# One program order for ScalarE, VectorE and PE through the expert part of a two-layer encoder

## The chip, the cores and the metric

The kernel is one program on one core of a Trainium2 chip. The metric is device time in microseconds from launch to end, the median over runs. Before the change it is 1147.02 us, the median of 3 runs (1145.33 to 1148.85).

Five engines matter. PE (TensorE) multiplies matrices and puts the results into the eight banks of PSUM; its weight loads are listed as PEld. ACT (ScalarE) and DVE (VectorE) copy, cast and combine tiles. SP (SyncE) issues the DMAs that bring data from device memory into SBUF. POOL (GpSimd) does little here. Each engine has its own list of instructions and takes them in the order in which the built program has them; an instruction that needs another engine's result waits on a semaphore, and all behind it on that engine wait with it.

## The reference

Two transformer layers over 256 tokens of width 1024, in float32: an even one (gated linear attention beside differential attention, then a SwiGLU feed-forward part), and an odd one (latent attention, then a mixture of eight SwiGLU experts). Only the odd layer's second half, the experts, is touched by the change:

```python
def _moe_swiglu(x, router_w, w_gate, w_up, w_down):
    t = x.reshape(B * S, D)                                  # 256 x 1024
    logits = (t @ router_w).astype(jnp.float32)
    top_vals, top_idx = lax.top_k(logits, TOP_K)             # 2 of 8
    w = jax.nn.softmax(top_vals, axis=-1)
    combine = jnp.einsum('nk,nke->ne', w, jax.nn.one_hot(top_idx, N_EXPERTS, dtype=jnp.float32))
    out = jnp.zeros_like(t)
    for e in range(N_EXPERTS):                               # w_gate, w_up 1024 x 2816, w_down 2816 x 1024
        out = out + combine[:, e:e + 1].astype(t.dtype) * _swiglu(t, w_gate[e], w_up[e], w_down[e])
    return out.reshape(B, S, D)
```

where `_swiglu(x) = (silu(x @ w_gate) * (x @ w_up)) @ w_down`. A layer norm over `ALPHA * x + out` follows and is the kernel's output.

## The kernel before, in words

**The experts as rounds.** The kernel sorts the experts by how many tokens chose them. The four fullest are *wide* (up to 128 token rows), the others *narrow* (up to 64). One-hot matrices P, made on DVE from the router's ranks (`one_hot`), gather each expert's rows on PE (`gather_pair`, `gather_narrow`; tiles ga, gn, xw, xn), and their transposes PT scatter the results back (`pt`, `e_scatter`, `n_tail`; tiles pt, sc, ns). Each expert's weights come as 33 chunks of 128 x 2048 floats (1 MB): 11 each of gate, up and down. The hidden width is done in six blocks b. The loop in `expert_steps` runs over rounds r: a round does block b of a wide expert (gate and up products, `e_gu`, tiles eg and eu), the down products of the wide block before (`e_down`, tile ey), the transposes of the hidden values (`e_tr`, `e_hT`: et, ehT), and then, two rounds behind (`BEHIND`), a narrow expert's blocks (`n_gu`, `n_down`, `n_tr`, `n_hT`: ng, nu, ny, nt). A full round takes six wide and six narrow chunks.

**The split.** A wide chunk is cut into a high part wh, rounded to the matmul's fast 32-bit form by a cast on ACT (helper line 126, CAST wh<-raw), and the rest wl, a subtraction on DVE (line 120, TENSOR_TENSOR wl<-raw,wh). Three products (`PASSES`) then make up one of nearly full precision: two with wh, and last the one with wl. Narrow chunks go to PE as they are. There are three buffers for wh (`SPLIT`), so at most three wide chunks stand split and unused; the next cast waits until PE is through with an older wh.

**What sets the order.** `run_steps` walks a list of steps. Ahead of a step's function it calls `advance`, which issues loads for all free slots and splits wide chunks up to ten keys ahead (`AHEAD`), as far as three buffers allow. SP's list is always in program order (`MANUAL`). In the router's stage a block `tc.manual_schedule(engines=ROUTE)` fixes PE, DVE and ACT too. In the expert part the wrapper `at` fixes only PE while a step's function runs (`EXPERT`). The lists of ACT and DVE there are ordered by the framework's scheduler, which works out when each operation should be ready and places it so. Side work (gathers, one-hot matrices, transposes, scatters) waits in a list `fillers`; `fill()` runs the next one, after a wide chunk's products and inside `e_down`.

**Loads.** A load goes to a free slot. Slots come free when PE has used a chunk. From the first narrow chunk on SP needs the sorted experts' numbers (tile who, made on DVE by `route_sort`).

Of the kernel before, what the change touches and what calls it, by code (L numbers as in the profile page):

```python
# [30 lines left out]
EXPERT = {mybir.EngineType.PE}  # L31
WSLOTS = 26
FBS = [512] * 5 + [256]

# [4 lines left out]
AHEAD = 10  # L39
# [53 lines left out]
def _build(tc, ctx, a, out):  # L93
# [35 lines left out]

    steps = []  # L130

    def step(fn, *keys, ahead=SPLIT - 1, own=0):

        steps.append((keys, fn, ahead, own))

    LATE = [("moe", 0, 0), ("moe", 0, 1)]
    slots = [(ring, f"raw{i}", 1) for i in range(RAW)]
# [63 lines left out]
    def run_steps():  # L201
# [91 lines left out]

        Q.update(take=take, advance=advance, late=load_late, load=lambda: advance(-1))
        at = 0
        for keys, fn, more, own in steps:
            n = len(keys) - own
            if keys:
                advance(at + max(more, n - 1))
            fn(*[cut.pop(at + j) for j in range(n)])  # L300
            for j in range(at, at + n):
                free(j)
            at += len(keys)

    def chunk():

# [42 lines left out]
    def norm_tile(r, h, st):  # L349
        V.bn_stats(st[1][:, h, :], r[:, h * 512:(h + 1) * 512])  # L350
# [1104 lines left out]
    def oo_last(*w):  # L1455
# [27 lines left out]
                r[t], st[t] = residual_tile(t), norm_begin()  # L1483
            residual(r[t], x2["x"], t, M["oo"][t], h)

        with tc.manual_schedule(engines=ROUTE):
            R["lp"] = [bank("lg") for _ in range(2)]
            for j in range(2):
                out_part("oo", 2 + j, 4, Z["A"], w[j], 0)
            for h in range(2):  # L1490
                res(0, h)
                norm_tile(r[0], h, st[0])
            out_part("oo", 2, 4, Z["A"], w[0], 1, (0,))
            for h in range(2):
                route_transpose(0, r[0], h)
            norm_stats(st[0])
            out_part("oo", 2, 4, Z["A"], w[0], 1, (1,))
            norm_first(r[0], r[0], st[0], ln, 0)
            route_shift(0, st[0])
            norm_first(r[0], r[0], st[0], ln, 1)  # L1500
            for h in range(2):
                norm_second(r[0], st[0], ln, h)
            for h in range(2):
                route_products(0, h)
            route_logits(0)
            route_rank(0)
            out_part("oo", 3, 4, Z["A"], w[1], 1, hfs=(0,))
            c1 = chunk()
            c1[0](0)
            c1[0](1)  # L1510
            out_part("oo", 3, 4, Z["A"], w[1], 1, hfs=(1,))
            route_before(0)
            slots.extend([(pers, "aH", 1), (pers, "aL", 1)])
            Q["load"]()
            res(1, 0)
            norm_tile(r[1], 0, st[1])
            route_slots(0)
            one_hot(0, 0, (0,))
            early.extend(bank("ga")[:, :128] for _ in range(4))
            route_transpose(1, r[1], 0)  # L1520
            gather(early[0], 0, 0)
            res(1, 1)
            route_transpose(1, r[1], 1)
            norm_tile(r[1], 1, st[1])
            norm_stats(st[1])
            c2 = chunk()
            norm_first(r[1], r[1], st[1], ln, 0)
            route_shift(1, st[1])
            route_products(1, 0)
            gather(early[1], 1, 0)  # L1530
            route_products(1, 1)
            gather(early[2], 2, 0)
            c2[0](0)
            route_logits(1)
            route_rank(1)
            early.extend(bank("ga")[:, :128] for _ in range(2))
            gather(early[3], 3, 0)
            route_before(1)
            for k in range(4, len(early)):
                gather(early[k], k, 0)  # L1540
            norm_second(r[1], st[1], ln, 0)
            route_slots(1)
            one_hot(0, 0, (1,))
            R["xw"] = R["p"].tile([128, 2, 8, 128], F32R, name="xw0", tag="xg0")
            for k in range(4):
                gather_end(k)
            norm_first(r[1], r[1], st[1], ln, 1)
            norm_second(r[1], st[1], ln, 1)
            SPARE.append(low_slot())
            slots.extend([(pers, "xtok1", 1, ("moe", 0, 0)), (pers, "ln", 1, ("moe", NE - 1, 11 + 4))])  # L1550
            for c in c1, c2:
                if c is c2:
                    c[0](1)
                c[1](0)
                c[1](1)
                c[2]()
# [407 lines left out]
    def expert_steps():  # L1964
        last = 6 * NW

        def at(fn, *keys):

            def run(*w):
                with tc.manual_schedule(engines=EXPERT):  # L1970
                    fn(*w)
            step(run, *keys, ahead=AHEAD)

        def wide_chunk(r, part, c):
            if not 0 <= r < last:
                return
            i, b = divmod(r, 6)
            if c not in chunks(b):
                return
            if part == 2:  # L1980
                at(lambda w: (e_down(b, c, w, (i, b), i, 1), fill()), W(i, 2, b, c))
            else:
                x = tuple((lambda k, q=q: R["xw"][:, q, k]) for q in range(2))
                at(lambda w: (e_gu(i, "gu"[part], b, c, w, x, (i, b)), fill()), W(i, part, b, c))

        def narrow_chunk(r, part, c):
            if not 0 <= r < last:
# [13 lines left out]
        def wide_begin(i, b):  # L2001
            if b == 0:
                fill(len(fillers) if i else 1)
                fillers.append(lambda: pt(i))

        def narrow_begin(i, b):
            if b == 0:
                fillers.append(lambda: pt(NW + i))
                if i + 1 < NW:
                    fillers.extend(lambda z=z: one_hot(i + 1, z) for z in range(2))  # L2010

        def gathers(i, b):
            if b == 5 and i + 1 < NW:
# [149 lines left out]
```

## Time and profile before

| | |
|---|---|
| median of 3 runs | 1147.02 us |
| the profiled execution | 1148.88 us, its span 1147.0 us, mean clock 0.985 |
| PE busy | 1094.4 us (95%) |
| DVE busy | 656.1 us (57%) |
| ACT busy | 520.8 us (45%) |
| expert loads | 263 of 1024 KB, median 8.7 us from issue to landing |

The span is from the first to the last instruction. Busy shares are over all stages. The router's stage starts near 405 us, the first expert product is at 430 us, the experts' last products end near 1134 us, and the final layer norm ends the program. PE is an almost unbroken row from 450 us on, so a microsecond counts only where PE stands still or runs at its lower clock.

### The profile page before, as it was taken

To read this page: it belongs to the slowest core of one execution; us is meant where nothing else is said; L and a number is where in the kernel's file an instruction comes from. 1 tells how busy PE (TensorE), PEld (TensorE's weight loads), DVE (VectorE), ACT (ScalarE), POOL (GpSimd) and SP (SyncE) were. 2 spreads that over 40 slices of the span, in tenths; PEclk is the share of its full clock that TensorE was granted. 3 is DMA by queue.
4 is the path that set the end of the run, shared out by engine and by line. 5 is a ranking of instruction groups with operands and counts; after the bars stand their busy time and mean duration, and the time that the engine had idled before them with its cause. 6 is when DMAs were issued, how large, how long until landed. Compare 5 with 4: busy or idle time off the path is not lost. (4 is left out here: it accounts for less than half of the span.)

```text
span 1147.0 us, 16462 instructions
## 1 busy us (share of the span) xinstructions
PE 1094.4 (95%) x6560; PEld 847.9 (74%) x6560; DVE 656.1 (57%) x784; ACT 520.8 (45%) x648; POOL 25.7 (2%) x42
## 2 busy tenths in 40 slices
PE   7999999999999989999999999999999999999994
PEld 6888788888878677877877776767766767777653
DVE  5777955554489576864346565456565456555323
ACT  5644554443368535743244534344444344444311
POOL 0101100000020010000000000000000000000000
PEclk9999999999999988999999999999999999999988
DMA  8832375555547435899999999999999999999961
GB/s 309 319 142 74 126 278 184 183 184 184 181 158 294 189 125 204 330 396 421 415 420 410 398 391 417 369 403 408 391 390 411 378 403 411 392 391 406 387 248 39
DMA packets 53153, 348.58 MB, mean 304 GB/s; under 512 B 7033, under 2 KB 8953, under 8 KB 12366
## 3 DMA queue, kind: packets, MB, share of 16 engines
q1 hardware_dynamic: 52318, 344.84, 76.9%
q0 software_dynamic: 752, 2.63, 0.7%
q8 instruction: 53, 0.87, 0.3%
q14 instruction: 30, 0.25, 0.1%
HBM read 346.37 MB, written 1.08 MB: 303 GB/s over the span
## 5 line engine op out<-in xcount | busy, mean ns | idle before, releaser
L120 DVE TENSOR_TENSOR wl<-raw,wh 128x2048 fp32r<-128x2048 f32 (+2 forms) x248 | 438.1, 1779 | 163.8 <-ACT wh L126 154.3
L126 ACT CAST wh<-raw 128x2048 fp32r<-128x2048 f32 (+2 forms) x222 | 336.0, 1550 | 146.0 <-PE fu L325 34.8
L120 DVE TENSOR_TENSOR xn<-xn,nu 128x256 f32<-128x256 f32 (+1 forms) x24 | 9.6, 399 | 176.6 <-PE nu L1892 176.6
L1799 PE MATMUL ey<-wh,ehT 128*128 128x512 f32 x352 | 99.1, 403 | 2.3 <-ACT wh L126 2.3
L1761 PE MATMUL eg<-wh,xw 128*128 128x512 f32 (+1 forms) x384 | 94.8, 390 | 1.2 <-ACT wh L126 1.2
L1761 PE MATMUL eu<-wh,xw 128*128 128x512 f32 (+1 forms) x384 | 89.6, 377 | 0.0
L1917 PE MATMUL ny<-raw,xn 128*64 128x256 f32 x704 | 87.7, 387 | 0.9 <-ACT xn L1907 0.9
L1892 PE MATMUL nu<-raw,xn 128*64 128x256 f32 (+1 forms) x768 | 83.6, 361 | 0.0
L1892 PE MATMUL ng<-raw,xn 128*64 128x256 f32 (+1 forms) x768 | 83.5, 362 | 0.0
L1761 PEld LDWEIGHTS eg<-wh,xw 128*128 128x128 f32 x384 | 66.5, 192 | 20.1 <-issue 6.9
L1761 PEld LDWEIGHTS eu<-wh,xw 128*128 128x128 f32 x384 | 67.7, 188 | 14.8 <-ACT eh L1771 1.0
L1799 PEld LDWEIGHTS ey<-wh,ehT 128*128 128x128 f32 x352 | 64.8, 190 | 15.3 <-ACT wh L126 2.5
L1917 PEld LDWEIGHTS ny<-raw,xn 128*64 128x64 f32 x704 | 50.3, 138 | 34.2 <-issue 11.2
L1892 PEld LDWEIGHTS ng<-raw,xn 128*64 128x64 f32 x768 | 55.5, 137 | 23.6 <-issue 0.4
L1892 PEld LDWEIGHTS nu<-raw,xn 128*64 128x64 f32 x768 | 55.2, 137 | 23.3 <-issue 0.4
L1896 ACT ACTIVATE xn<-ng 128x256 f32<-128x256 f32 (+1 forms) x24 | 8.8, 367 | 130.9 <-PE ng L1892 130.9
L1799 PE MATMUL ey<-wl,ehT 128*128 128x512 f32 x176 | 57.1, 406 | 4.0 <-DVE wl L120 4.0
L1761 PE MATMUL eg<-wl,xw 128*128 128x512 f32 (+1 forms) x192 | 49.9, 385 | 9.6 <-DVE wl L120 9.6
L126 ACT CAST ehT<-et 128x512 fp32r<-128x512 f32 (+1 forms) x24 | 13.2, 551 | 92.2 <-PE ey L1799 85.5
L1761 PE MATMUL eu<-wl,xw 128*128 128x512 f32 (+1 forms) x192 | 49.6, 383 | 0.8 <-DVE wl L120 0.2
L1761 PEld LDWEIGHTS eg<-wl,xw 128*128 128x128 f32 x192 | 33.0, 188 | 21.7 <-DVE wl L120 15.9
L1799 PEld LDWEIGHTS ey<-wl,ehT 128*128 128x128 f32 x176 | 31.7, 189 | 17.7 <-DVE wl L120 9.7
(369 smaller groups left out, 1622.1 us busy)
## 6 DMA issues: line engine op xcount, KB each, us to landing
raw<-wmoe SPq DMA_DIRECT2D x263, 1024.0 KB, 8.7
raw<-wpre SPq DMA_DIRECT2D x55, 1024.0 KB, 5.0
raw<-wpre SPq DMA_DIRECT2D x2, 896.0 KB, 4.5
xtok<-xT SPq DMA_DIRECT2D x4, 256.0 KB, 4.7
raw<-wpre SPq DMA_DIRECT2D x2, 512.0 KB, 7.5
xtok<-x SPq DMA_DIRECT2D x1, 1024.0 KB, 7.1
ln<-ln_gain SPq DMA_DIRECT2D x2, 512.0 KB, 8.0
ln<-ln_bias SPq DMA_DIRECT2D x2, 512.0 KB, 11.1
```

The costliest lines, as they stand in the source:

```text
L120: V.tensor_tensor(out=o, in0=i0, in1=i1, op=op)
L126: A.copy(H, src)
L1761: PE.matmul(o, x[i](4 * c + k), w[j][:, k * cols:(k + 1) * cols], start=(c, i, j, k) == (0, 0, 0, 0), stop=(c, i, j, k) == (nch - 1, *PASS ...
L1799: PE.matmul(E["y", ytag][hf], hT[i][:, fs], w[j][:, ws], start=(b, c, i, j, k) == (0,) * 5, stop=last and (i, j, k) == (*PASSES[2], 1))
L1892: PE.matmul(E[n, "n"][half(h), :m], x_narrow(i)[:, 4 * c + k], w[:, k * cols + h * m:k * cols + h * m + m], start=(c, k) == (0, 0), stop=( ...
L1896: A.activation(E["nh"][:, :m], E[n, "n"][:, :m], AF.Silu)
L1917: PE.matmul(E["y", NW + i][half(hf), q * 256:q * 256 + 256], h, w[:, k * D + o:k * D + o + 256], start=(b, c, k, q) == (0,) * 4, stop=(b, ...
```

## The change

The function that ends the router's stage (`oo_last`) no longer closes its `ROUTE` block: it opens it by hand, and the last step of the expert part closes it. ACT, DVE and PE therefore keep the order in which the code names their operations until the last expert is done. A step gets a second function, `then`. Its order becomes: the split of its own chunk if it is missing, the products with their evictions, the freeing of slots, `advance` (loads, and the next splits), and then the side work. The transposes PT are made two blocks later, and the start of the accumulator (`accumulate`) moves from the head of round 5 into round 4, behind the narrow down products.

```diff
-    def step(fn, *keys, ahead=SPLIT - 1, own=0):
-        steps.append((keys, fn, ahead, own))
+    def step(fn, *keys, ahead=SPLIT - 1, own=0, then=None):
+        steps.append((keys, fn, ahead, own, then))
...
-        for keys, fn, more, own in steps:
+        for keys, fn, more, own, then in steps:
             n = len(keys) - own
             if keys:
-                advance(at + max(more, n - 1))
+                advance(at + (n - 1 if then else max(more, n - 1)))
             fn(*[cut.pop(at + j) for j in range(n)])
             for j in range(at, at + n):
                 free(j)
             at += len(keys)
+            if then:
+                if keys:
+                    advance(at + more)
+                then()
...
-        with tc.manual_schedule(engines=ROUTE):
-            R["lp"] = [bank("lg") for _ in range(2)]
+        R["order"] = tc.manual_schedule(engines=ROUTE)
+        R["order"].__enter__()
+        R["lp"] = [bank("lg") for _ in range(2)]
...
-        def at(fn, *keys):
-            def run(*w):
-                with tc.manual_schedule(engines=EXPERT):
-                    fn(*w)
-            step(run, *keys, ahead=AHEAD)
+        def at(fn, *keys, then=lambda: None):
+            step(fn, *keys, ahead=AHEAD, then=then)
...
-                at(lambda w: (e_down(b, c, w, (i, b), i, 1), fill()), W(i, 2, b, c))
+                at(lambda w: e_down(b, c, w, (i, b), i, 1), W(i, 2, b, c), then=fill)
...
-                at(lambda w: (e_gu(i, "gu"[part], b, c, w, x, (i, b)), fill()), W(i, part, b, c))
+                at(lambda w: e_gu(i, "gu"[part], b, c, w, x, (i, b)), W(i, part, b, c), then=fill)
...
             if b == 0:
                 fill(len(fillers) if i else 1)
+            elif b == 2:
                 fillers.append(lambda: pt(i))
...
-            if r == 5:
-                step(accumulate)
...
                 if part == 2:
                     wide(n - 1, narrow_end)
+                    if r == 4:
+                        at(accumulate)
...
-    step(lambda: fill(len(fillers)))
+    step(lambda: (fill(len(fillers)), R["order"].__exit__(None, None, None)))
```

On ACT, the program before has this piece from round 6 to round 7 (eh and xn<-ng are the SiLU of a wide and of a narrow gate, y and ehT evictions of the down products and of the transposes; the wh casts are the splits):

```order
L1771 ACTIVATE eh<-eg_5068 128x512
L126 CAST wh_5099<-raw_4801 128x2048
L126 CAST wh_5121<-raw_4842 128x2048
L126 CAST y_5197<-ey_4017 128x512
L126 CAST y_5197<-ey_4018 128x512
L126 CAST ehT<-et_5189 128x512
L1896 ACTIVATE xn<-ng_5245 128x256
L126 CAST wh_5143<-raw_5030 128x2048
L126 CAST wh_5168<-raw_5044 128x2048
L1907 COPY xn<-nt_5327 128x256
L126 CAST wh_5210<-raw_5064 128x2048
L1771 ACTIVATE eh<-eg_5307 128x512
```

The changed program has, in the same place:

```order
L1777 ACTIVATE eh<-eg_4771 128x512
L125 CAST wh_4809<-raw_4591 128x2048
L125 CAST wh_4828<-raw_4747 128x2048
L125 CAST wh_4847<-raw_4758 128x2048
L125 CAST wh_4865<-raw_4769 128x2048
L125 CAST y_4874<-ey_3967 128x512
L125 CAST y_4874<-ey_3968 128x512
L125 CAST ehT<-et_4869 128x512
L1902 ACTIVATE xn<-ng_4901 128x256
L125 CAST wh_4960<-raw_4784 128x2048
L1913 COPY xn<-nt_4968 128x256
L1777 ACTIVATE eh<-eg_4945 128x512
```

Two of the three casts that stood behind the narrow gate's SiLU now stand four places and more ahead of it.

On DVE, around the first narrow one-hot matrix (P<-iota,ms, tile P_3560; ms, cap, cnt are small results of the sorting of experts), before:

```order
L120 TENSOR_TENSOR wl_3843<-raw_3154,wh_3842 128x2048
L1654 TENSOR_REDUCE ms<-msd 128x8
L1682 TENSOR_SCALAR mxc<-mxc 128x1
L120 TENSOR_TENSOR eh<-eh,eu_3815 128x512
L120 TENSOR_TENSOR msd<-perm,mr 128x64
L1683 CAST cnt<-mxc 128x1
L1694 TENSOR_SCALAR P_3560<-iota,ms 128x128
L1654 TENSOR_REDUCE ms<-msd 128x8
L120 TENSOR_TENSOR wl_3894<-raw_3216,wh_3893 128x2048
L1694 TENSOR_SCALAR P_3560<-iota,ms 128x128
```

and in the changed program:

```order
L1660 TENSOR_REDUCE ms<-msd 128x8
L1683 TENSOR_SCALAR scap<-srank 128x8
L1684 TENSOR_SCALAR scap<-scap 128x8
L119 TENSOR_TENSOR slack<-scap,sl_3685 128x8
L1687 TENSOR_REDUCE mxc<-slack 128x1
L1688 TENSOR_SCALAR mxc<-mxc 128x1
L1689 CAST cnt<-mxc 128x1
L119 TENSOR_TENSOR wl_3798<-raw_3152,wh_3797 128x2048
L1700 TENSOR_SCALAR P_3560<-iota,ms 128x128 x2
L119 TENSOR_TENSOR wl_3819<-raw_3154,wh_3818 128x2048
L119 TENSOR_TENSOR eh<-eh,eu_3803 128x512
```

The split of the fifth chunk (raw_3152) and all of the sorting now precede both halves of P; the splits of raw_3154 and raw_3216 come after it.

On PE in the same stretch (eu is the up product of round 0, gn the narrow gather that reads P_3560), before:

```order
L1761 MATMUL eu_3815<-wh_3658,xw_3617 128x512 x8
L1761 MATMUL eu_3815<-wl_3659,xw_3617 128x512 x4
L1761 MATMUL eu_3815<-wh_3713,xw_3617 128x512 x8
L1761 MATMUL eu_3815<-wl_3714,xw_3617 128x512 x4
L1723 MATMUL gn_3828<-P_3560,lnr_3472 128x64
L1723 MATMUL gn_3861<-P_3560,lnr_3472 128x64
L1781 MATMUL et_3877<-ident,eh 128x128 x4
```

and in the changed program:

```order
L1767 MATMUL eu_3803<-wh_3669,xw_3617 128x512 x8
L1767 MATMUL eu_3803<-wl_3670,xw_3617 128x512 x4
L1729 MATMUL gn_3822<-P_3560,lnr_3472 128x64 x8
L1767 MATMUL eu_3803<-wh_3673,xw_3617 128x512 x8
L1767 MATMUL eu_3803<-wl_3674,xw_3617 128x512 x4
L1729 MATMUL gn_3852<-P_3560,lnr_3472 128x64 x8
L1787 MATMUL et_3862<-ident,eh 128x128 x4
```

Half of the narrow gather now stands ahead of the fourth chunk's products instead of behind them.

## Rows read from the trace of the kernel before

**Rows 1.** Busy us (and instructions) per engine, then PEclk, DMA share, GB/s; single rounds.

```profile
521.68:549.71 28.03, 28.03 (x176) 20.84 (x174) 13.17 (x8) 12.87 (x10) 0.00 (x0) 1.00 1.01 419
692.14:721.96 29.82, 28.87 (x177) 20.66 (x175) 15.28 (x9) 12.75 (x11) 0.00 (x0) 1.00 1.01 422
549.71:577.25 27.54, 27.54 (x206) 22.55 (x204) 8.41 (x10) 8.62 (x15) 0.00 (x0) 1.00 1.01 417
721.96:751.39 29.43, 28.11 (x206) 22.49 (x204) 11.76 (x11) 11.15 (x17) 0.00 (x0) 1.00 0.91 361
577.25:752.39 175.14, 170.30 (x1079) 125.63 (x1078) 92.81 (x71) 75.97 (x71) 0.00 (x0) 1.00 0.99 400
```

**Rows 2.** Whom PE waited for, 575 to 1097 us: total us, times, longest.

```profile
PE eg L1761 <- DVE wl L120: 9.6, 17, 0.9
PE ey L1799 <- DVE wl L120: 4.0, 9, 0.8
PE eg L1761 <- ACT wh L126: 1.2, 3, 0.4
```

**Rows 3.** Groups, 575 to 1097 us: busy us, mean ns, idle before and its releaser.

```profile
L120 DVE TENSOR_TENSOR wl<-raw,wh 128x2048 fp32r<-128x2048 f32 x99 | 226.6, 2289 | 38.7 <-ACT wh L126 35.7
L126 ACT CAST wh<-raw 128x2048 fp32r<-128x2048 f32 x99 | 183.8, 1905 | 0.0
```

**Rows 4.** Timeline at round 7's start: start us, us, instruction, [idle before <-releaser].

```profile
600.60 0.38 ACT L1896 ACTIVATE xn<-ng 128x256 f32<-128x256 f32 x1 [5.55 <-PE ng L1892]
600.88 3.69 ACT L126 CAST wh<-raw 128x2048 fp32r<-128x2048 f32 x2
...
604.12 0.42 DVE L120 TENSOR_TENSOR xn<-xn,nu 128x256 f32<-128x256 f32 x1 [8.24 <-PE nu L1892]
604.46 4.67 DVE L120 TENSOR_TENSOR wl<-raw,wh 128x2048 fp32r<-128x2048 f32 x2
...
606.80 1.20 PE L1761 MATMUL eg<-wl,xw 128*128 128x512 f32 x4 [0.73 <-DVE wl L120]
```

**Rows 5.** Whom PE waited for, 1097 to 1131 us.

```profile
PE ey L1799 <- ACT wh L126: 2.3, 1, 2.3
```

**Rows 6.** As rows 1: two stretches at the lower granted clock.

```profile
444.32:451.15 6.83, 6.16 (x23) 5.49 (x23) 5.45 (x18) 0.59 (x1) 0.33 (x1) 0.50 0.58 215
1099.68:1106.51 6.83, 5.82 (x17) 3.26 (x18) 2.29 (x1) 0.96 (x1) 0.00 (x0) 0.50 1.00 414
```

**Rows 7.** Timeline of DVE, the router's end and round 0.

```profile
419.45 0.23 DVE L120 TENSOR_TENSOR df<-df,rconst 128x64 f32<-128x64 f32 x1
419.71 0.22 DVE L1608 TENSOR_REDUCE rk<-df 128x8 f32<-128x64 f32 x1
...
420.86 2.28 DVE L120 TENSOR_TENSOR wl<-raw,wh 128x2048 fp32r<-128x2048 f32 x1
423.06 0.28 DVE L1699 TENSOR_SCALAR P<-iota,mr 128x128 fp32r<-128x128 f32 x1
...
432.00 0.81 DVE L120 TENSOR_TENSOR xw<-ga,xw 128x128 fp32r<-128x128 f32 x3
...
444.65 0.28 DVE L1694 TENSOR_SCALAR P<-iota,ms 128x128 fp32r<-128x128 f32 x1
```

**Rows 8.** Timeline of PE in round 0.

```profile
430.18 2.33 PE L1761 MATMUL eg<-wh,xw 128*128 128x512 f32 x8
...
436.50 2.02 PE L1761 MATMUL eu<-wh,xw 128*128 128x512 f32 x8
...
439.29 2.02 PE L1761 MATMUL eu<-wh,xw 128*128 128x512 f32 x8
...
444.99 1.12 PE L1723 MATMUL gn<-P,lnr 128*128 128x64 f32 x4 [2.75 <-DVE P L1694]
```

**Rows 9.** Timeline of ACT in round 0.

```profile
437.70 1.28 ACT L1771 ACT_TABLE_LOAD   x1
439.00 0.60 ACT L1771 ACTIVATE eh<-eg 128x512 f32<-128x512 f32 x1
```

More of the change, by code (lines that the diff above doesn't have):

```diff
@@ L30 @@
 ROUTE = {mybir.EngineType.PE, mybir.EngineType.DVE, mybir.EngineType.Activation}
-EXPERT = {mybir.EngineType.PE}
 WSLOTS = 26
@@ L1484, in res @@
             residual(r[t], x2["x"], t, M["oo"][t], h)
-        with tc.manual_schedule(engines=ROUTE):
-            R["lp"] = [bank("lg") for _ in range(2)]
[L1488 to L1556, printed above, removed]
@@ new lines, in oo_last @@
+        R["order"] = tc.manual_schedule(engines=ROUTE)
+        R["order"].__enter__()
+        R["lp"] = [bank("lg") for _ in range(2)]
+        for j in range(2):
+            out_part("oo", 2 + j, 4, Z["A"], w[j], 0)
+        for h in range(2):
+            res(0, h)
+            norm_tile(r[0], h, st[0])
+        out_part("oo", 2, 4, Z["A"], w[0], 1, (0,))
+        for h in range(2):
+            route_transpose(0, r[0], h)
+        norm_stats(st[0])
+        out_part("oo", 2, 4, Z["A"], w[0], 1, (1,))
@@ new lines, in oo_last @@
+        norm_first(r[0], r[0], st[0], ln, 0)
+        route_shift(0, st[0])
+        norm_first(r[0], r[0], st[0], ln, 1)
+        for h in range(2):
+            norm_second(r[0], st[0], ln, h)
+        for h in range(2):
+            route_products(0, h)
+        route_logits(0)
+        route_rank(0)
+        out_part("oo", 3, 4, Z["A"], w[1], 1, hfs=(0,))
+        c1 = chunk()
+        c1[0](0)
+        c1[0](1)
+        out_part("oo", 3, 4, Z["A"], w[1], 1, hfs=(1,))
+        route_before(0)
@@ new lines, in oo_last @@
+        slots.extend([(pers, "aH", 1), (pers, "aL", 1)])
+        Q["load"]()
+        res(1, 0)
+        norm_tile(r[1], 0, st[1])
+        route_slots(0)
+        one_hot(0, 0, (0,))
+        early.extend(bank("ga")[:, :128] for _ in range(4))
+        route_transpose(1, r[1], 0)
+        gather(early[0], 0, 0)
+        res(1, 1)
+        route_transpose(1, r[1], 1)
+        norm_tile(r[1], 1, st[1])
+        norm_stats(st[1])
+        c2 = chunk()
+        norm_first(r[1], r[1], st[1], ln, 0)
@@ new lines, in oo_last @@
+        route_shift(1, st[1])
+        route_products(1, 0)
+        gather(early[1], 1, 0)
+        route_products(1, 1)
+        gather(early[2], 2, 0)
+        c2[0](0)
+        route_logits(1)
+        route_rank(1)
+        early.extend(bank("ga")[:, :128] for _ in range(2))
+        gather(early[3], 3, 0)
+        route_before(1)
+        for k in range(4, len(early)):
+            gather(early[k], k, 0)
+        norm_second(r[1], st[1], ln, 0)
+        route_slots(1)
+        one_hot(0, 0, (1,))
@@ L1558, in oo_last @@
+        R["xw"] = R["p"].tile([128, 2, 8, 128], F32R, name="xw0", tag="xg0")
+        for k in range(4):
+            gather_end(k)
+        norm_first(r[1], r[1], st[1], ln, 1)
+        norm_second(r[1], st[1], ln, 1)
+        SPARE.append(low_slot())
+        slots.extend([(pers, "xtok1", 1, ("moe", 0, 0)), (pers, "ln", 1, ("moe", NE - 1, 11 + 4))])
+        for c in c1, c2:
+            if c is c2:
+                c[0](1)
+            c[1](0)
+            c[1](1)
+            c[2]()
         fillers.extend([gather_rest, route_sort, lambda: one_hot(0, 1), lambda: gather_narrow(0),
@@ L2003, in wide_begin @@
                 fill(len(fillers) if i else 1)
+            elif b == 2:
                 fillers.append(lambda: pt(i))
         def narrow_begin(i, b):
-            if b == 0:
+            if b == 0 and i + 1 < NW:
+                fillers.extend(lambda z=z: one_hot(i + 1, z) for z in range(2))
+            elif b == 2:
                 fillers.append(lambda: pt(NW + i))
-                if i + 1 < NW:
-                    fillers.extend(lambda z=z: one_hot(i + 1, z) for z in range(2))
         def gathers(i, b):
```

## The prediction

> **What bounds the kernel now.** I read the page's slices first, to see that PE is full from 450 us on and the DMA engines nearly so, then the stretches between rounds, then whom PE waits for, and last the timeline around one wait.
>
> The stretches give the first surprise [rows 1]. A full round of the first expert takes 28.03 us, and PE is busy in all of it. The same round of the second expert has the same work (176 and 177 matmul records) and takes 29.82 us, of which PE is busy for 28.87. For the round with a last block it is 27.54 against 29.43 us. So the later rounds lose 1.8 to 1.9 us each for something that is not work. It isn't the transfers: the slow round has 422 GB/s, the fast one 419, and the slow last-block round has a DMA share of only 0.91.
>
> Whom PE waits for between 575 and 1097 us says what it is [rows 2]: nothing but splits. 26 waits are on DVE's low part, 3 on ACT's high part, 14.8 us in all. The groups say whether these splits were late because their data was [rows 3]: none of the 99 casts of that stretch had ACT idle in front of it, so no cast was waiting at the head of ACT's list for a landing, and DVE's subtractions waited 35.7 us for the casts alone. The timeline shows where the casts were instead [rows 4]. At round 7's start ACT stands idle for 5.55 us in front of the narrow gate's SiLU, which waits for PE; right behind it, at 600.88, two casts run back to back. DVE stands idle for 8.24 us in front of the narrow product and then does two subtractions. PE has run the wide chunk's first eight products by then and waits 0.73 us for the low part. Both engines had time; the splits stood behind instructions that could not run.
>
> **The change part by part: the steady stretch.** In program order a split follows at once the wide chunk whose buffer it inherits, so with three buffers the next three chunks are split before a round's narrow part begins. In the piece of ACT's list shown, four casts stand ahead of the narrow SiLU instead of two, and one behind it instead of three. For the wait of [rows 4] that means: both chunks at the head of round 7 are cut before PE gets there. What a round asks of DVE is six subtractions of 2.29 us [rows 3], some 14 us, and up to 3 us of accumulation, of 28 us; ACT has less. So nothing else is late next, and the 14.8 us of waits go.
>
> They are worth more than their idle time, since a wait also breaks the overlap of neighbouring matmuls. The two pairs of rounds measure it [rows 1]: 1.79 us lost at 0.95 us idle, and 1.89 at 1.32, a factor of 1.9 and of 1.4. The ends are 14.8 us (idle alone) and 28 us (1.9 times). I take the smaller factor, since the round it is from has more of the waits: 21 us.
>
> **The tail.** The last wide chunk's cast also stands behind narrow evictions, and PE waits 2.3 us for it [rows 5]. The granted clock falls to 0.50, the 1.2 GHz level, for 6.83 us around that wait, and PE is busy for 5.82 of them [rows 6]; at full clock the same work takes half, 2.9 us less. In program order this cast stands before the narrow SiLU of the round ahead, so both go: 5 us. The ends are 2.3 us (the clock falls anyway) and 5.2.
>
> **The start.** Here program order is worse. Four steps:
>
> 1. Before the gathers DVE does a subtraction of 2.28 us right in front of the one-hot matrix P [rows 7]. It moves behind the gathers, and P comes up to 2.2 us earlier. I take 1.7 of it (its ends are 0 and 2.2), since the first eight products took 2.33 us where later ones take 2.02 [rows 8], so PE was not yet at full clock and gives some back: the first expert product comes at 428.5 instead of 430.18 [rows 8], and DVE is through with the gathered tiles at 431.1 instead of 432.8 [rows 7].
> 2. The narrow one-hot matrix now stands behind three splits and the whole sorting of experts. 431.1, two splits (4.6), 18 small operations at 0.26 us each, the distance of two dependent ones [rows 7] (4.7), one more split (2.3) and both halves (0.5): 443.2. Before, the first half started at 444.65 [rows 7].
> 3. PE now meets the gather one chunk earlier, at 439.29 - 1.7 = 437.6, and waits some 5.6 us for P, where before it had done the fourth chunk first and waited 2.75 us, to 444.99 [rows 8]. A chunk is 439.29 - 436.50 = 2.8 us [rows 8], so PE gets to the same point at 443.2 + 2.8 = 446.0: 1 us late. A stretch of 6.83 us at the lower clock follows the wait in the kernel before [rows 6]; I expect one after this wait too, at the same price.
> 4. The router's softmax moves from before the first wide SiLU to between two of them. That costs ACT two more table loads of 1.28 us [rows 9], 2.6 us, and puts 15 small operations, 3.9 us, between the splits of the eighth and the ninth chunk. The cover is three chunks of 2.8 us less the split itself (1.9 on ACT, 2.3 on DVE): 4.2 us. So 6.5 - 4.2 = 2.3 us show on PE.
>
> The loss is 3 us. Its ends are a gain of 2 us (steps 2 to 4 hidden, step 1 whole) and a loss of 7 (one more half-clock stretch, 3.4 us).
>
> On step 4 the profile and the skill differ. The cast ends when the table load begins, and the SiLU starts 0.02 us after its end [rows 9], so a switch costs 1.28 us by this trace. The Trainium skill, "ScalarE: Activation LUTs", section "What ACT_TABLE_LOAD costs", adds a drain of about 1.38 us to each switch. By that the sum would be 2.8 us higher, 1127 us; the trace decides, and I leave it out.
>
> The later transposes PT and the moved accumulator cost nothing: both are on ACT (under 2 us), at places where three split chunks lie ahead of PE. SP's list has the same loads in the same order, and the experts' numbers, for which it waits, come earlier with step 2.
>
> **The sum.** Made against the profiled execution: its span is 1147.0 us, 1147.0 - 21 - 5 + 3 = 1124. That execution took 1148.88 us in all, 1.9 us over the median of the runs, so the same subtraction from the median 1147.02 gives 1124 us as well.
>
> **The rivals.**
>
> *Only the idle time comes back.* The overlap at a wait is not gained, the clock falls in the tail as before, the start costs its 3 us: 1147 - 14.8 - 2.3 + 3 = 1133 us. For it: the factor is from two pairs of rounds. Against: both pairs agree that it is over 1.
>
> *The transfers take over.* An expert pair's 66 loads are 69.2 MB. At 420 GB/s [rows 1] they take 165 us; a wide expert takes 175.1 us now, some 168 without the waits. The margin is 3 us, and in a full round the loads (12.6 MB at 419 GB/s, 30 us) are already slower than PE (28 us). If the mean of 400 GB/s [rows 1] is all that can be kept up, an expert takes 173 us, 2 less than now: 1147 - 6 - 5 + 3 = 1139 us. Against: 417 to 422 GB/s stand in three of four rounds, and no cast waited for a landing [rows 3].
>
> *Program order blocks in its turn.* The transposes et stand between two down chunks and need the wide product eh from DVE. If a split in front of eh has to wait for its cast, and the cast for a buffer, PE waits at et in each of the 24 rounds, for up to a whole split: 24 x 2.29 = 55 us, less the 23 gained, 1179 us. From 1 us per round on the change is slower. For it: an idle engine with runnable work behind its head is just what [rows 4] shows. Against: an eviction stands ahead of its own step's split, and PE ran the first expert's rounds without idle time, with splits early in DVE's list there too. The Trainium skill, "PSUM — Partial Sum Buffer", section "Engine vs sequencer instructions", calls the queues of ACT and DVE strict FIFO, which is this rival's ground; the trace agrees with it at 600 us.
>
> *The casts can't move.* If it is the three buffers of wh that hold them and not the list, only the start's 3 us remain: 1147 + 3 = 1150, or about the same as now if the start costs nothing. Against: at 600.88 two casts run back to back as soon as the SiLU is through [rows 4].
>
> **How the numbers follow.** The forecast has 0.65, its own range being 1114 (28 us in the steady stretch, start without loss) to 1131. Only the idle time: 0.15. Transfers: 0.08. Blocking: 0.06. Casts that can't move: 0.06, half of it within 0.3%. About 0.3% (3.4 us) is what a measurement of this kernel can tell from no change. Faster by more: 0.65 + 0.15 + 0.08 = 0.88; the same 0.04, with a little for a start much dearer than thought; slower 0.08. For 8 in 10 the range goes from 1116 to 1138, which leaves out the last two rivals, most of the transfers' case, and the forecast's lowest end.
>
> **What would show it.** Right: the waits of PE on wl and wh between the second expert's start and the last falls from 14.8 us to under 3; full rounds take 28.0 and last-block rounds 27.5 us in every expert; no stretch at 0.50 near the last wide chunk; at the start a wait of 4 to 6 us of the narrow gather on P, and two table loads around the softmax. Wrong: rounds that stay at 29.8 us; casts with idle time in front of them that a landing ended, and a DMA share of 1.0 in every round (transfers); or waits of et on eh in each round (blocking).

## The result and the profile after

The changed kernel takes 1113.45 us (median of 4 runs, 1111.93 to 1114.27), the kernel before, run beside it, 1146.57 us: a ratio of 0.971, with a 95% interval of 0.969 to 0.973. The gain is 33 us where 23 were predicted, and the time lies under the range of 1116 to 1138. In the profiled executions the span falls from 1147.0 to 1111.2 us, by 35.8; the sums below are made against these.

First the rounds, as in [rows 1]. Columns: stretch, its us, then busy us (and records) of PE, PE's weight loads, DVE, ACT and POOL, then granted clock, DMA share, GB/s. A full round of the first and of the second expert, the two rounds with a last block, and the second expert whole:

```profile
523.20:551.50 28.30, 28.30 (x178) 21.03 (x176) 15.29 (x9) 15.08 (x12) 0.00 (x0) 1.00 1.01 419
688.02:716.30 28.28, 28.28 (x179) 21.07 (x177) 15.29 (x9) 13.24 (x11) 0.00 (x0) 1.00 1.01 420
551.50:579.04 27.54, 27.54 (x206) 22.55 (x204) 11.69 (x11) 10.96 (x16) 0.00 (x0) 1.00 1.01 410
716.30:743.85 27.55, 27.55 (x206) 22.55 (x205) 11.78 (x11) 10.75 (x16) 0.00 (x0) 1.00 1.01 418
579.04:743.85 164.81, 164.74 (x1075) 125.37 (x1074) 92.67 (x69) 75.76 (x70) 0.00 (x0) 1.00 1.01 419
```

The second expert's rounds are now as long as the first one's, PE is busy in all of them, and the second expert takes 164.81 us instead of 175.14. Whom PE waits for between 575 and 1097 us (total us, times, longest) answers [rows 2]; no split is left in the list:

```profile
PE nt L1909 <- DVE xn L119: 1.1, 2, 0.6
PE ny L1923 <- ACT xn L1913: 0.9, 2, 0.5
PE ns L1958 <- ACT ny L1952: 0.7, 1, 0.7
```

The groups answer [rows 3]. There no cast had idle time in front of it; now the casts are early and wait themselves, mostly for PE to give a buffer back:

```profile
L119 DVE TENSOR_TENSOR wl<-raw,wh 128x2048 fp32r<-128x2048 f32 x97 | 222.1, 2290 | 125.4 <-ACT wh L125 121.2 <-DMA raw<-wmoe 2.3
L125 ACT CAST wh<-raw 128x2048 fp32r<-128x2048 f32 x97 | 184.0, 1908 | 131.5 <-PE eg L1767 72.0 <-PE ey L1805 33.3 <-DMA raw<-wmoe 14.4
```

And the timeline at the start of round 7 answers [rows 4]. Behind the narrow SiLU and the narrow product no split is due, and the products with the low part (606.30) follow those with the high part without a wait; the next cast waits 5.12 us for PE:

```profile
600.99 0.38 ACT L1902 ACTIVATE xn<-ng 128x256 f32<-128x256 f32 x1 [4.62 <-PE ng L1898]
...
604.33 2.13 PE L1767 MATMUL eg<-wh,xw 128*128 128x512 f32 x8
604.51 0.42 DVE L119 TENSOR_TENSOR xn<-xn,nu 128x256 f32<-128x256 f32 x1 [5.30 <-PE nu L1898]
...
606.30 1.09 PE L1767 MATMUL eg<-wl,xw 128*128 128x512 f32 x4
606.50 1.91 ACT L125 CAST wh<-raw 128x2048 fp32r<-128x2048 f32 x1 [5.12 <-PE eg L1767]
```

Where the 35.8 us came from can be read from three stretches with the same records in both kernels. From round 6 to the start of round 23, before and then after:

```profile
577.25:1072.34 495.09, 480.73 (x3017) 351.72 (x3015) 265.18 (x188) 214.81 (x195) 0.00 (x0) 1.00 0.99 399
```

```profile
579.04:1045.58 466.54, 466.45 (x3017) 353.53 (x3015) 265.61 (x192) 216.71 (x194) 0.00 (x0) 1.00 1.01 419
```

That is 28.55 us, and it has two halves: 14.3 us less idle time on PE (14.36 to 0.09), and 14.28 us less *busy* time for the same number of matmul records, 3017. From round 23 to the end, again before and after:

```profile
1072.34:1147.00 74.66, 55.41 (x423) 37.89 (x421) 26.41 (x37) 13.37 (x20) 1.96 (x2) 0.89 0.51 201
```

```profile
1045.58:1111.20 65.62, 49.85 (x423) 36.59 (x421) 19.53 (x34) 10.81 (x18) 1.96 (x2) 0.94 0.63 253
```

9.04 us less; the stretch at 0.50 around the last wide chunk [rows 6] is gone. The start gives back 1.79 us: round 6 begins at 579.04 instead of 577.25. 28.55 + 9.04 - 1.79 = 35.8.

At the start these rows answer [rows 7, 8]; the one on DVE is the narrow one-hot matrix P. The gather of the narrow tokens waits for it as foreseen, and the next products run at the lower clock (3.43 us where others take 2.02):

```profile
426.60 2.10 PE L1767 MATMUL eg<-wh,xw 128*128 128x512 f32 x8
...
440.83 0.48 DVE L1700 TENSOR_SCALAR P<-iota,ms 128x128 fp32r<-128x128 f32 x2
441.16 3.68 PE L1729 MATMUL gn<-P,lnr 128*128 128x64 f32 x16 [5.52 <-DVE P L1700]
444.60 3.43 PE L1767 MATMUL eu<-wh,xw 128*128 128x512 f32 x8
```

### The profile page after: what moved, and what is told of

The parts are those of the page before. It is cut to its first block, busy times and chain, and to the rows that moved or that the text cites. A ratio compares the mean times of both kernels' runs of the same rounds, so it can differ in the third digit from the quotient of the medians.

```text
span 1111.2 us, 16461 instructions
## 1 busy us (share of the span) xinstructions
PE 1073.6 (97%) x6560; PEld 846.8 (76%) x6560; DVE 656.0 (59%) x784; ACT 524.8 (47%) x650; POOL 23.7 (2%) x42
## 5 line engine op out<-in xcount | busy, mean ns | idle before, releaser
L125 ACT CAST wh<-raw 128x2048 fp32r<-128x2048 f32 (+2 forms) x222 | 339.4, 1551 | 275.6 <-PE eg L1767 83.5
L1923 PE MATMUL ny<-raw,xn 128*64 128x256 f32 x704 | 81.3, 382 | 0.9 <-ACT xn L1913 0.9
L1898 PE MATMUL ng<-raw,xn 128*64 128x256 f32 (+1 forms) x768 | 80.2, 361 | 0.0
L1898 PE MATMUL nu<-raw,xn 128*64 128x256 f32 (+1 forms) x768 | 80.1, 361 | 0.0
L1898 PEld LDWEIGHTS ng<-raw,xn 128*64 128x64 f32 x768 | 53.1, 137 | 23.9 <-issue 0.4
L1805 PE MATMUL ey<-wl,ehT 128*128 128x512 f32 x176 | 54.8, 392 | 1.0 <-DVE wl L119 1.0
L1777 ACT ACTIVATE eh<-eg 128x512 f32<-128x512 f32 (+1 forms) x24 | 13.5, 562 | 58.9 <-PE eg L1767 58.9
L1767 PEld LDWEIGHTS eu<-wl,xw 128*128 128x128 f32 x192 | 34.2, 188 | 7.2
```

The source lines that it names most:

```text
L125: A.copy(H, src)
L1767: PE.matmul(o, x[i](4 * c + k), w[j][:, k * cols:(k + 1) * cols], start=(c, i, j, k) == (0, 0, 0, 0), stop=(c, i, j, k) == (nch - 1, *PASS ...
L1777: A.activation(E["h", tag][:, :cols], o, AF.Silu)
L1805: PE.matmul(E["y", ytag][hf], hT[i][:, fs], w[j][:, ws], start=(b, c, i, j, k) == (0,) * 5, stop=last and (i, j, k) == (*PASSES[2], 1))
L1898: PE.matmul(E[n, "n"][half(h), :m], x_narrow(i)[:, 4 * c + k], w[:, k * cols + h * m:k * cols + h * m + m], start=(c, k) == (0, 0), stop=( ...
L1923: PE.matmul(E["y", NW + i][half(hf), q * 256:q * 256 + 256], h, w[:, k * D + o:k * D + o + 256], start=(b, c, k, q) == (0,) * 4, stop=(b, ...
```

## The experiments

My theory at this point: what held the splits was ScalarE's list, in which casts stood behind narrow evictions; the low parts only followed. Rivals: VectorE's own list; the order within a step. Three kernels differ from the changed one in the engines that keep program order in the expert part. `oo_last` ends with these lines, in the second kernel with `DVE` in the place of `Activation` and in the third with PE alone:

```diff
+        R["order"].__exit__(None, None, None)
+        R["order"] = tc.manual_schedule(engines={mybir.EngineType.PE, mybir.EngineType.Activation})
+        R["order"].__enter__()
```

### ScalarE in program order, VectorE not

> The changed kernel, but in the expert part only PE and ScalarE keep program order; VectorE's list is again set by the scheduler. Theory A (the casts decide: ScalarE's list held them behind narrow evictions, VectorE's low parts only followed): no PE wait on a split from the second expert on, 1113 to 1118 us. Rival B (VectorE's own list decides): the low parts stand behind evictions again, most of the gain is lost, 1135 to 1147 us. At the start the narrow one-hot matrix comes later in VectorE's list than in the changed kernel, so either theory allows 2 to 4 us more there.

Measured: 1119.67 us, ratio to before 0.977 (0.974 to 0.980), 1.7 us over the range of theory A and far under that of rival B. No wait on a split is left, and from round 6 on all rounds but one are those of the changed kernel. Round 10 has the exception:

```profile
689.01:724.05 35.04, 30.94 (x179) 22.93 (x177) 18.77 (x15) 13.34 (x11) 0.00 (x0) 0.90 0.97 384
```

In it the scheduler put four one-hot operations ahead of a split. VectorE stood still for 13.13 us before them, until PE's transposes pt were through, and the narrow transposes waited for the narrow product behind them:

```profile
692.32 0.48 DVE L1708 TENSOR_SCALAR P<-iota,ms 128x128 fp32r<-128x128 f32 x2 [13.13 <-PE pt L1756]
...
693.11 2.28 DVE L119 TENSOR_TENSOR wl<-raw,wh 128x2048 fp32r<-128x2048 f32 x1
...
695.91 0.41 DVE L119 TENSOR_TENSOR xn<-xn,nu 128x256 f32<-128x256 f32 x1
```

```profile
696.38 0.69 PE L1912 MATMUL nt<-ident,xn 128*128 128x128 f32 x2 [4.10 <-DVE xn L119]
696.72 3.76 PE L1770 MATMUL eg<-wh,xw 128*128 128x512 f32 x8
```

One wait of 4.10 us makes the round 35.04 instead of 28.28 us: the clock falls behind it (eight products 3.76 us instead of 2.1), and it costs 6.8. Without that round the kernel would stand within 1 us of the changed one. Theory A holds for the waits on splits, rival B falls; VectorE's program order is worth little more than the one wait of round 10.

### VectorE in program order, ScalarE not

> The changed kernel, but in the expert part only PE and VectorE keep program order; ScalarE's list is set by the scheduler, which puts three casts ahead of a round's narrow transposes where program order has five. Theory A (casts decide): the low parts wait for late casts, and what stands behind them on VectorE waits too, 1140 to 1160 us. Rival B (VectorE's list decides): 1113 to 1120 us.

Measured: 1183.97 us, ratio 1.033 (1.030 to 1.035), 24 us beyond the range of theory A. Program order blocks here, as one rival of the prediction said: the engine that takes work over has a fixed list and the one that hands it over has not. But it does so in another way than that rival had it. There et waited for eh in each round for up to 2.29 us; here PE waits for VectorE 11 times between round 6 and round 23, 8 times for the narrow product (29.1 us in all) and 3 times at et (16.2 us). Round 11's beginning, ACT and then DVE, then PE:

```profile
734.39 0.38 ACT L1780 ACTIVATE eh<-eg 128x256 f32<-128x256 f32 x1 [2.50 <-PE eg L1770]
734.68 3.69 ACT L125 CAST wh<-raw 128x2048 fp32r<-128x2048 f32 x2
```

```profile
736.60 2.29 DVE L119 TENSOR_TENSOR wl<-raw,wh 128x2048 fp32r<-128x2048 f32 x1 [1.80 <-ACT wh L125]
738.81 0.68 DVE L119 TENSOR_TENSOR ehT<-et,ehT 128x512 fp32r<-128x512 f32 x1
739.41 0.41 DVE L119 TENSOR_TENSOR xn<-xn,nu 128x256 f32<-128x256 f32 x1
```

```profile
739.87 0.69 PE L1912 MATMUL nt<-ident,xn 128*128 128x128 f32 x2 [5.51 <-DVE xn L119]
740.21 3.76 PE L1770 MATMUL eu<-wh,xw 128*128 128x256 f32 x16
```

The cast stands behind the wide SiLU on ACT. VectorE must do that chunk's low part first, and the narrow product, for which everything was ready, stands two places behind it. So PE waits 5.5 us for an eviction that has nothing to do with the cast, and the products behind it run at the lower clock (sixteen in 3.76 us).

### PE alone in program order, the new step kept

> The changed kernel with its new step (split after the products, side work after the split, the moved transposes and accumulator), but in the expert part only PE keeps program order, as in the kernel before. Theory A: the step alone is worth nothing, 1144 to 1150 us. Rival C (the order within a step carries the gain, the engines' program order little): 1115 to 1130 us. Sizing: before had 14.8 us of PE idle time and 33.7 us of idle time on the weight loads' row (49 waits) at splits between 575 and 1097 us, and 28.6 us of time came back; if the load row is the right measure, this run and the two others stand in time to the changed kernel as their load rows' waits do, within 3 us; if PE's own idle row times 1.4 is, they stand 20 to 40% lower than that.

Measured: 1148.87 us, ratio 1.0018 (1.0007 to 1.0029). The new step without the two other lists gains nothing; rival C falls. Round 6 begins at 580.25, 3.0 us later than in the kernel before, and here too PE meets the narrow gather ahead of the fourth chunk and waits 4.97 us for P. So the loss at the start needs no program order on ScalarE or VectorE. It comes with the new step or with PE's order, which here is kept over the whole expert part and before only within a step's function; the two were not told apart. The reverse, the old step with all three engines in program order, was not run, so what the new step adds to the gain is open.

The sizing is less clear than I had put it. 3017 records again from round 6 to 23 take

```profile
580.25:1073.42 493.17, 477.62 (x3017) 350.30 (x3016) 262.65 (x187) 212.47 (x194) 0.00 (x0) 1.00 0.99 399
```

26.63 us more than in the changed kernel, at 15.55 us idle: a factor of 1.7. The weight loads' row has 35.0 us of waits on splits there. PE's order is that of the changed kernel here, so the distances between the starts of neighbouring products can be compared. From the last product with a high part to the first with the low part they are 20.6 us longer in all, between the products with the low part 4.8, and into a round's first product 1.6: 27.0 us, which is the whole loss within half a microsecond. It all lies at splits.

### One wait a round

To get the price of a wait by itself, the first wide split of a round is held until the narrow product of the round before is issued:

```diff
+        def held(key):
+            return (key[0] == "moe" and key[1] < NW and key[2] < 11 and key[2] % 2 == 0
+                    and 6 * key[1] + key[2] // 2 > max(2, R.get("nu", -1) + 3))
...
+                if held(order[j]):
+                    break
...
                 tt(E["nh"][:, :m], E["nh"][:, :m], E[n, "n"][:, :m], OP.mult)
+                R["nu"] = 6 * i + b
```

> The changed kernel with one wait put back in each round from round 3 on (21 rounds): the split of a round's first wide chunk, and of those after it, is held until the narrow product of the round before stands in VectorE's list; both engines keep program order. PE comes to the low part 2.0 us after the narrow product's end, the low part is made 0.42 + 2.29 = 2.7 us after it, so about 0.7 us of idle time on PE per round and no other wait, 14 to 15 us in all. The price of a wait: its idle time alone, 1127 to 1129 us; 1.4 times (as put in the prediction), 1132 to 1135 us; about twice (as all 47 waits of the kernel before cost together, 28.55 us at 14.4 us idle), 1140 to 1144 us.

Measured: 1135.45 us, 22 us over the changed kernel and 0.5 us over what the factor 1.4 was to give. Round 9 of this kernel, and then of the changed one:

```profile
663.88:695.39 31.51, 30.77 (x192) 21.91 (x191) 17.82 (x13) 12.95 (x11) 0.00 (x0) 1.00 0.99 394
```

```profile
657.51:688.02 30.51, 30.51 (x193) 22.06 (x191) 17.83 (x13) 13.17 (x10) 0.00 (x0) 1.00 1.01 419
```

And the wait in it, PE's weight load and PE:

```profile
666.74 0.76 PEld L1774 LDWEIGHTS eg<-wl,xw 128*128 128x128 f32 x4 [1.18 <-DVE wl L119]
666.74 1.20 PE L1774 MATMUL eg<-wl,xw 128*128 128x512 f32 x4 [0.74 <-DVE wl L119]
```

One wait costs 1.00 us: 0.74 of idle time and 0.26 of longer busy time. Some 0.1 of the 0.26 can be seen in the row: four products with the low part take 1.20 us behind the wait and 1.09 without one. The rest is lost overlap: a product's record lasts 0.40 us, but the next one starts 0.23 us after it when nothing waits. From round 6 to 23 the kernel has 13.44 us of idle time and loses 18.41: a factor of 1.4, as the prediction had it. The kernel before has nearly the same idle time, 14.36 us, and loses 28.55. So the factor on idle time is not a constant; what differs is the number of waits, below.

### Where the next bound is

> The changed kernel without the products of the activations' high part with the weights' low part in the wide experts' gate and up (the splits are still made, the loads are the same): about 24 us of PE's work less per expert, by the groups of the changed kernel. If PE alone is the bound: 96 us less, some 1017 us. If the transfers are as good as the bound (66 loads at 420 GB/s are 165 us an expert, the last landing 28 us before the end now): an expert still takes 163 to 165 us from round 6 on, the time is 1095 to 1105 us, and PE waits for landings or for casts that wait for landings.

The edit is `for i, j in PASSES[:1] + PASSES[2:]` in `e_gu`. What it leaves out is the second pass, the activations' low part with the weights' high part, and not the pair that the expectation names; both passes have the same number of products. One execution took 1102.28 us. The transfers hold it: from round 6 to 23 it takes 464.87 us (466.54 in the changed kernel) at the same rate while PE is busy for 424 of them, and the casts wait 100.4 us for landings between 583 and 1050 us (14.4 in the changed kernel). PE itself waits mostly at et for eh, 32.6 us, which stands behind the late splits in VectorE's list. First the whole stretch, then the casts:

```profile
570.03:1034.90 464.87, 423.73 (x2746) 307.22 (x2744) 264.24 (x193) 215.14 (x193) 0.00 (x0) 0.97 1.01 420
```

```profile
L125 ACT CAST wh<-raw 128x2048 fp32r<-128x2048 f32 x94 | 177.4, 1904 | 167.3 <-DMA raw<-wmoe 100.4 <-PE eg L1767 45.3 <-PE ey L1805 15.3
```

So taking away work of PE that was put at 96 us brings 11 us, and 9.0 of these before round 6, which begins at 570.03. From round 6 to 23 the changed kernel stands with PE and transfers equal, at 164.8 and 165 us an expert.

### Mending the start

> The changed kernel with two moves at the start: the narrow gather one chunk later (an empty place in the list of side work), so that PE does the fourth chunk's products while VectorE makes the one-hot matrix, and the softmax's exponential before the first wide SiLU, which takes one table load and its wait out of the casts. If PE is still the bound (10 us and more between landing and use at the end): the 5.5 us wait and about 1.8 us of later waits go, some 0.9 us comes back as a wait of the transposes on eh: 5 to 6 us, 1107 to 1109 us. Rival D (the transfers already set the end, at 165 us an expert): the gain is under 1.5 us, 1112 to 1114 us.

```diff
-        fillers.extend([gather_rest, route_sort, lambda: one_hot(0, 1), lambda: gather_narrow(0),
+        fillers.extend([lambda: (gather_rest(), route_exp()), route_sort, lambda: one_hot(0, 1), lambda: None,
+                        lambda: gather_narrow(0),
```

(`route_exp` is the first half of `route_weights`, up to the exponential.) Measured: 1111.52 us, ratio 0.969 (0.967 to 0.972), not told apart from the changed kernel's 0.969 to 0.973. The forecast of 1107 to 1109 us failed, and rival D's 1112 to 1114 was not met either. The wait on P shrank from 5.52 to 3.92 us only, since P stands late in VectorE's list whatever PE does first, and the lower clock followed it all the same:

```profile
442.20 3.67 PE L1732 MATMUL gn<-P,lnr 128*128 128x64 f32 x16 [3.92 <-DVE P L1703]
...
446.38 3.76 PE L1770 MATMUL eg<-wh,xw 128*128 128x512 f32 x8
```

> The changed kernel with only the softmax's exponential (and the four small VectorE operations in front of it) moved ahead of the first wide SiLU. It tests the fourth step at the start, which was priced at 2.3 us. If that price is right: 1111 to 1111.7 us. If the three split chunks cover the two table loads and only the waits of 0.95 and 0.87 us that the changed kernel shows behind them are at stake: 1111.7 to 1112.7 us. If even these come from the small VectorE operations, which stay where they are: 1113 to 1114 us.

The exponential alone: 1113.18 us, ratio 0.971 (0.970 to 0.973): no difference that the times can tell. The trace tells more. The changed kernel's waits of 0.95 us on a low part and of 0.87 us on eh, both in round 1, are gone, and round 1 takes 2.3 us less for the same 79 records, first in the changed kernel and then here:

```profile
450.89:470.35 19.46, 17.64 (x79) 13.87 (x78) 15.27 (x24) 13.63 (x12) 0.26 (x1) 1.00 0.81 311
```

```profile
451.46:468.63 17.17, 17.17 (x79) 13.98 (x78) 14.67 (x20) 10.99 (x9) 0.26 (x1) 1.00 0.88 332
```

But the wait on P grew from 5.5 to 6.6 us, and round 0 is 1.1 us longer. In this execution, the fastest of the five, round 6 begins at 577.25 us, 1.8 earlier than in the changed kernel.

> The changed kernel with the start in another order: the experts are sorted and the narrow one-hot matrix is made right behind the gathered tiles, ahead of the splits of the third chunk on; the exponential comes behind the second chunk's, and the narrow gather behind the third and the fourth chunk. Theory E (the start's loss is VectorE's order: sorting and one-hot matrix stand behind splits that nobody needs yet): no wait of the gather on P, waits of up to 1 us and 0.5 us on the third and fourth chunk's low parts instead, round 1 begins near 444 us instead of 450.9, no stretch at 0.50 in it: 5 to 8 us, 1105 to 1109 us. Rival D (the transfers set the end): under 1.5 us beyond the run with the gather one chunk later, 1110 to 1112 us. Rival F (the wait moves on to eh and the splits of round 1, as in the run before): 1109 to 1112 us, with waits on eh or wl over 3 us in round 0 or 1.

```diff
+        fillers.extend([lambda: (gather_rest(), route_sort(), one_hot(0, 1)), route_exp, lambda: None,
+                        lambda: gather_narrow(0), lambda: gather_narrow(4), route_weights])
```

1110.11 us, ratio 0.969 (0.967 to 0.970), above theory E's range; round 1 begins at 450.02 us and not near 444. The wait on P is gone, but rival F has its share, if with waits under the 3 us that it named: 2.0 us on the third chunk's low part, 1.5 us on eh. ScalarE's list was held by the exponential for 8.58 us, so that casts came late:

```profile
440.35 0.20 ACT L1639 ACTIVATE v<-v 128x2 f32<-128x2 f32 x1 [8.58 <-DVE v L119]
```

> The start of the run with the sorting first, mended where its trace shows new waits: the exponential stands ahead of the gathered tiles' copies (there it held ScalarE's list for 8.6 us), and the six small operations for the capacity come later. Theory E: at most 1 us of wait on the third chunk's low part, round 1 begins 4 to 5 us earlier than there, 1105 to 1107 us. Rival F (the wait moves on again, to eh or the splits of round 1): 1108 to 1110 us. Rival D (transfers): 1109.5 to 1110.5 us, with casts or narrow products that wait for landings at the end.

```diff
         one_hot(0, 0, (1,))
+        route_exp()
...
+        fillers.extend([lambda: (gather_rest(), route_sort(), one_hot(0, 1)), lambda: None, lambda: None,
+                        lambda: gather_narrow(0), lambda: gather_narrow(4), lambda: (route_cap(), route_weights())])
```

(`route_cap` is the last part of `route_sort`, the small operations for the capacity.) 1105.16 us, ratio 0.964 (0.963 to 0.966), as theory E had it. PE's first round has no wait at all (15.86 us busy of 15.87), and round 1 begins at 444.70.

> As the run before, and the second half of the layer norm's last two operations ahead of the gathered tiles' low parts, since the rest of the gather waits 2.1 us for it in every run so far. If PE's way to the first product is what counts: 1.5 to 2 us less than the run before, 1103 to 1105 us. If VectorE's queue there is full anyway and only changes order: the same as the run before within 0.7 us.

```diff
+        norm_first(r[1], r[1], st[1], ln, 1)
+        norm_second(r[1], st[1], ln, 1)
         for k in range(4):
             gather_end(k)
-        norm_first(r[1], r[1], st[1], ln, 1)
-        norm_second(r[1], st[1], ln, 1)
```

1102.84 us, ratio 0.962 (0.961 to 0.964): the fastest version, 10.6 us under the changed kernel. The first product comes at 423.06 us instead of 428.83 in the run before, but a wait of 1.8 us on the third chunk's low part, and products at the lower clock behind it, take most of that back: round 1 begins at 443.52 instead of 444.70.

```profile
432.66 1.19 PE L1776 MATMUL eu<-wl,xw 128*128 128x512 f32 x4 [1.82 <-DVE wl L119]
...
436.48 3.76 PE L1776 MATMUL eu<-wh,xw 128*128 128x512 f32 x8
```

Only its start differs from the changed kernel: round 6 begins at 570.36 us, 8.7 earlier, and from there to round 23 both take the same 466.5 us. Rival D is out for these steps: the profiled span is 8.7 us shorter too (1102.5 us).

## Why the predicted gain came out low

**What bounds the kernel** was read rightly: the splits were late for their place in two lists and for nothing else. Each sign named for it came: no wait on a split, rounds alike in all experts (rounds 10, 16 and 22 take 28.28, 28.29 and 28.25 us), no lower clock near the last wide chunk, 5.5 us of wait on P, two table loads around the softmax. The first experiments add that ScalarE's list is the one that gains, that VectorE's order adds some 6 us to it, and that VectorE must not have program order alone.

**The steady stretch** is the step that failed: the factor 1.4 on PE's idle time, chosen between 1.4 and 1.9 because "the round it is from has more of the waits". It gave 21 us; 28.55 came, a factor of 2.0 on the 14.36 us and so more than either of the two. The mechanism was right, the size was not, and the run with one wait a round shows why a factor is the wrong form. The wait measured there costs its idle time and 0.26 us more. And many waits show no idle time on PE at all, since a matmul's record lasts longer than the distance to the next one; they show on the weight loads. For the kernel before, from round 6 to 23:

```profile
PEld eg L1761 <- DVE wl L120: 15.2, 16, 1.3
PEld ey L1799 <- DVE wl L120: 8.5, 14, 1.3
...
PEld eu L1761 <- DVE wl L120: 6.2, 14, 0.6
...
PEld eg L1761 <- ACT wh L126: 1.9, 3, 0.7
```

47 waits, where PE's own row has 28. Idle time 14.36 us and 47 times 0.26 make 26.6 us; 28.55 were gained. For PE alone in program order the same sum, 15.55 us and 51 waits, gives 28.8 where 26.63 were lost; for one wait a round, 13.44 us and 20 waits on splits, 18.6 where 18.41 were. It is good to some 2 us, no better: the extra per wait lies between 0.22 and 0.30 us. Waits of another kind have another price: the run with one wait a round has 11 more on that row, of the transposes on eh (3.9 us), which are not in the 20 and lengthened the products' distances by 1.1 us in all. The load row's own 31.8 and 35.0 us are 10 to 30% too much.

A second sign had been on the record: I put a wide expert without waits at 168 us, from the first expert's later rounds. It takes 164.8: its rounds 6 to 8, with the last blocks of the wide and the narrow expert before, take 25.3, 26.5 and 26.7 us. So the loss per expert was 10.3 us and not 7.

**The tail** was worth 9.0 us and not 5, if it is taken from the start of round 23: 5.6 us less busy and 3.5 us less idle. The wait of 2.3 us and the stretch at the lower clock went as foreseen. Of the idle time 2.3 us are that wait and some 1.2 are waits on splits within round 23, which the prediction had in its first term; how the busy time divides between the two was not measured.

**The start** came out at a loss of 1.8 us to round 6 where 3 were put. Step by step: the first product came at 426.60 and not 428.5 (step 1 was too small by 1.9 us). The lower clock ahead of it lasted 3.42 us instead of 10.24, and the last twelve gathers took 1.60 us instead of 2.93. Both halves of P were done at 441.31 and not 443.2: DVE was through with the gathered tiles at 430.45 instead of 431.1, and what stands between took 1.2 us less than step 2 had it. PE's wait was 5.52 where 5.6 were put, and the stretch at 0.50 came behind it (step 3 right). Step 4, the softmax's 2.3 us, is what the run with the early exponential shows: round 1 takes 2.3 us less there. Its two table loads stand in the trace, and the SiLU starts 0.02 us after the second one's end, so no drain follows the switch here either:

```profile
458.07 1.28 ACT L1777 ACT_TABLE_LOAD   x1
459.37 0.60 ACT L1777 ACTIVATE eh<-eg 128x512 f32<-128x512 f32 x1
```

That the time of that run did not change is no sign against step 4, since the longer wait on P and the scatter of the runs (1111.62 to 1114.04 us) hide it.

**The rivals.** That the transfers take over was right in its floor (165 us an expert) and wrong in its price: the casts do wait for landings now, 14.4 us, and the DMA share is 1.01 in every round, which I had named as this rival's sign. PE doesn't wait for it, as a cast has the time of two or three chunks. A sign on the transfer's side alone says nothing before PE's own row shows it. Program order that blocks was real in the kernel where VectorE alone has it. That its 1183.97 us stand near the 1179 put for this rival is luck: the price was 24 waits of 2.29 us at et, and the run has 8 of 5.4 to 5.5 us, five of them for the narrow product, with the lower clock behind them, 63.8 us in all from round 6 to 23 (530.38 against 466.54).

## What to carry to other kernels

When a producer and its consumer run on two engines (here cast and subtraction), give both lists the same order: the consumer's alone made the kernel 3.3% slower, the producer's alone 2.3% faster, both 2.9%. Size a wait of the matmul engine by comparing a slow stretch with one that has the same records and no waits, and by the count of waits on the weight loads' row, not by the idle time of the matmul row. And look where freed time ends: here the steady stretch stopped just where the transfers' rate stands, so it was the start that still had time to give, 10.6 us of it.

## What the runs showed of the hardware

- A wait of 0.74 us between two groups of products added 0.26 us to the busy time of the round; with one a round the granted clock stayed at 1.00.
- The waits of 3.92 to 5.52 us shown above, and one of 1.82 us, were followed by products at about half speed (3.4 to 3.8 us for eight instead of 2.1); one of 4.10 us cost 6.8 in its round.
- A switch of ScalarE's table cost its load of 1.28 us; the SiLU started 0.02 us after it.
- The transfers held 419 to 420 GB/s over some 466 us, with PE at 100% and at 91% busy alike.
